# Expert products on TensorE in the order of their weights, and the sums of x and the expert outputs on VectorE, each tile's transposes beside its sums

## The chip, the cores and the metric

One core of a Trainium2 chip runs the whole kernel. The metric is device time in microseconds. The kernel before took 1904.27 us as the median of three runs (1900.39 to 1905.04); less is better.

## The reference, cut to what matters

Two transformer blocks run one after the other on 512 tokens of width 1024, in fp32. The change lies at the seam between them: the mixture of experts that ends the first block, the sum of its output with x, and the normalisation with which the second block begins.

```python
def hierarchical_moe(h, ...):
    ...
    for e in range(N_EXPERTS):
        hid = jax.nn.silu(jnp.matmul(h, w_gate[e])) * jnp.matmul(h, w_up[e])
        out = out + jnp.matmul(hid, w_down[e]) * combine[:, e:e + 1]
    return out

    m = hierarchical_moe(h2, ...)
    return x + m.reshape(b, s, d)          # end of the first block
    ...
    h = rms_norm(x, norm_gain[l])          # start of the second block
    cols = h @ w_in_a[j]
    ...
    mem_out = memory_cross_attention(q_mem, mem, ..., w_mem_kv[l], ...)
```

There are 32 experts. A token goes to two of them, so its output is the sum of two rows, and x + m is a sum of three terms.

## The kernel before, in words

Products of full precision are split in three: each fp32 operand is written as a high and a low part (names `whi`, `wlo` for weights, `hh`, `hl` for activations), and `mm3` (lines 368 to 372) issues three matmuls, high by high (L370), low by high (L371), high by low (L372). The high part of a weight unit is made by ScalarE (L229), the low part by VectorE or GpSimd (L232). The experts' products are the exception: they take the raw fp32 weights.

All weights come from HBM through one class, `Stream`. A plan lists the units (mostly 512 KB) in the order of use, SyncE issues their loads as soon as a slot of the unit's lane is free (L217), and `ws.get` hands them out in the order of the plan. The lanes have names such as `mraw`, `hraw`, `xraw`, `praw`; in the expert loop they hold dozens of units at the start and, towards the end, mainly those of `mraw` (twelve slots), `hraw` and `xraw`. Slots of `xraw` are also where the four tiles of x (`x<-x1d`, L1468) are put after the loop, and slots of `mraw` hold the tiles `m` and `gF` of the stage behind it.

**The expert loop** (lines 1448 to 1464). Experts are handled in 16 pairs; 64 tokens of the one and 64 of the other share a tile of 128. For a pair, `gather_tokens` (L1374 to L1384) fetches the tokens' rows by an indirect DMA from GpSimd, scales them on VectorE (L1377), transposes them on TensorE (eight transposes, L1382) and copies them back (L1384). `gate_up` (L1397) uses eight weight units in four steps u0 to u3; `hidden` (L1402 to L1404) forms the gated product `th` on ScalarE and VectorE; `turned` (L1410) transposes it twice; `down` (L1423) uses four units, in two halves that ScalarE (L1427) and VectorE (L1425) copy to `y`, of which there are two tiles; GpSimd then scatters `y` by rows to `yd` in HBM (L1428). The weights are planned in the order: units 0 to 7 of pair j+1, then units 8 to 11 of pair j. So `gate_up` of the next pair comes ahead of `down` of this one. The program is written in that order too, with the gather of pair j+1 ahead of its own `gate_up`, but on TensorE a scheduler picks the final order by its own estimates.

**After the loop.** A count decides whether up to fourteen additional pairs are needed. `values_load` (L1511) brings it into a register of every engine (a TENSOR_LOAD on each), and a branch (L1516) skips the additional code; with this data it is always skipped. Behind the branch each engine goes on in the second section of the program, and the order there on TensorE, ScalarE, VectorE and GpSimd is the written one (`manual_schedule`):

- `vB_steps`, 16 `mm3` of the memory tokens with the value weights, of which `AFTER[0]` steps are issued ahead of the loads of `m` and the rest behind.
- SyncE loads eight tiles from `yd`: `ms[c]` (L1530) and `ms2[c]` (L1531), the two expert rows of the tokens of tile c. They wait until the last scatter is in HBM.
- `kv`, 16 `mm3` with the key weights (`acc<-whi,mT`), dealt out by the numbers of `AFTER`.
- for each tile c of 128 tokens: `x2[c] += ms2[c]` on GpSimd (L1537), `x2[c] += ms[c]` on VectorE (L1538), and the sum of squares of the result on ScalarE (L1542). ScalarE and GpSimd also split the first four weight units of the second block in between (`kraw`, L229 and L232).
- at c = 3, `transposed` turns all four tiles: six transposes for each tile into six PSUM banks (L401), then the other eight (L409), each followed by the high and low part (`hh` by L383, `hl` by L384). The first product of the second block is `sc<-whi,hh`.

## Time and profile before

| what | value |
|---|---|
| median of three runs | 1904.27 us (1900.39 to 1905.04) |
| the profiled execution | 1904.58 us |
| its span, first to last instruction | 1902.8 us |
| mean granted TensorE clock | 0.976 of full speed |
| busy share | TensorE 95%, VectorE 47%, ScalarE 39%, GpSimd 20% |
| bytes moved | 261.17 MB |

The profiled execution lies 0.3 us above the median. All times below are counted from the start of its span. The expert loop's first product comes at 491 us and its last ends at 744 us, and the second block's first product stands at 811 us. The stage between, in which x + m is formed, is the one in which TensorE idles most: a page that calls it 95% busy overall says little about it.

### The profile page before, as it was taken

The numbers are of one execution on the slowest core, as the hardware profiler recorded it, in microseconds if no ns is written. First come the engines' busy times: TensorE is split into PE (matmuls) and PEld (weight loads), VectorE is DVE, ScalarE is ACT, GpSimd is POOL, SyncE is SP. The second block draws the span as 40 slices with busy tenths as digits, with TensorE's granted clock in tenths as the row PEclk, the third lists the DMA queues.
The fourth block names the chain that finished last, engine by engine and source line by source line (L and its number), as shares of the span: only waits on it lengthen the run. The fifth ranks groups of instructions, "written<-read, shape, count | busy, mean of one in ns | idle before, by whom it ended". The sixth has DMA issues, their size and how long they took to land.

```text
span 1902.8 us, 25340 instructions
## 1 busy us (share of the span) xinstructions
PE 1806.9 (95%) x9426; PEld 1384.7 (73%) x9426; DVE 888.2 (47%) x1876; ACT 733.6 (39%) x1754; POOL 378.4 (20%) x467
## 2 busy tenths in 40 slices
PE   8999999998997787499999999999999999999999
PEld 8857766786432223389989889989888877777887
DVE  4389756276322231262243332243466426677571
ACT  5475355243100111243454433454454333233460
POOL 1301200010210101422533302433300001222200
PEclk9999999999999798799999999999999999999999
DMA  5221222187999996442222212222223322112231
GB/s 176 78 67 34 72 69 81 50 279 275 380 415 412 412 399 234 157 136 89 89 67 89 67 45 92 85 67 89 67 89 112 133 66 92 65 58 66 67 111 56
DMA packets 83685, 261.17 MB, mean 137 GB/s; under 512 B 12896, under 2 KB 14688, under 8 KB 83552
## 3 DMA queue, kind: packets, MB, share of 16 engines
q1 hardware_dynamic: 78080, 248.43, 36.9%
q0 software_dynamic: 4608, 8.40, 1.2%
q10 hardware_dynamic: 864, 2.62, 0.3%
q8 instruction: 77, 1.26, 0.3%
q14 instruction: 56, 0.46, 0.1%
HBM read 248.92 MB, written 18.87 MB: 141 GB/s over the span
## 4 chain that ended last, share of the span: by engine, by line
PE 56%; DVE 2%; issue 1%; ACT 1%; POOL 1%; POOLq 0%; ACTq 0%
PE acc L370 14%; PE acc L371 13%; PE acc L372 13%; PE sc L370 2%; PE sc L372 2%; PE sc L371 2%; PE sc L1916 1%; PE sc L1712 1%; PE tp L1653 1%; PE sc L1715 1%; PE tp L1720 1%; PE oT L1729 1%; PE oT L1964 1%; POOL x L1537 0%; PE oT L1724 0%
## 5 line engine op out<-in xcount | busy, mean ns | idle before, releaser
L370 PE MATMUL acc<-whi,hh 128*128 128x512 f32 (+2 forms) x936 | 383.0, 411 | 1.4 <-ACT hh L383 0.6
L371 PE MATMUL acc<-wlo,hh 128*128 128x512 f32 (+2 forms) x936 | 372.6, 399 | 0.0
L372 PE MATMUL acc<-whi,hl 128*128 128x512 f32 (+2 forms) x936 | 371.8, 400 | 0.0
L232 DVE TENSOR_TENSOR wlo<-wraw,whi 128x1024 fp32r<-128x1024 f32 (+4 forms) x209 | 244.9, 1175 | 252.0 <-ACT whi L229 251.2
L229 ACT ACTIVATE whi<-wraw 128x1024 fp32r<-128x1024 f32 (+4 forms) x239 | 239.2, 1002 | 296.8 <-PE acc L371 115.8
L370 PEld LDWEIGHTS acc<-whi,hh 128*128 128x128 f32 x936 | 223.5, 239 | 28.0 <-issue 2.8
L371 PEld LDWEIGHTS acc<-wlo,hh 128*128 128x128 f32 x936 | 224.1, 240 | 22.1 <-issue 1.7
L372 PEld LDWEIGHTS acc<-whi,hl 128*128 128x128 f32 x936 | 222.9, 239 | 21.6
L370 PE MATMUL acc<-hh,whi 128*128 128x512 f32 x448 | 184.7, 412 | 0.0
L372 PE MATMUL acc<-hh,wlo 128*128 128x512 f32 x448 | 177.7, 397 | 0.0
L371 PE MATMUL acc<-hl,whi 128*128 128x512 f32 x448 | 176.8, 395 | 0.0
L232 POOL TENSOR_TENSOR wlo<-wraw,whi 128x1024 fp32r<-128x1024 f32 (+3 forms) x30 | 70.6, 2353 | 526.6 <-ACT whi L229 452.2
L365 POOL TENSOR_TENSOR rs<-rsa,mhalf 128x4 f32<-128x4 f32 (+1 forms) x80 | 79.2, 990 | 325.7 <-DVE rsa L362 269.3
L1397 PE MATMUL acc<-mraw,xgt 128*64 128x512 f32 x232 | 103.0, 649 | 6.5 <-DMA mraw<-in_w_moe 5.5
L704 ACT ACTIVATE hjk<-acc 128x128 bf16<-128x128 f32 x232 | 64.1, 276 | 104.2 <-PE acc L372 73.2
L370 PEld LDWEIGHTS acc<-hh,whi 128*128 128x128 f32 x448 | 84.5, 189 | 21.2 <-issue 4.9
L372 PEld LDWEIGHTS acc<-hh,wlo 128*128 128x128 f32 x448 | 84.2, 188 | 19.8 <-issue 1.0
L371 PEld LDWEIGHTS acc<-hl,whi 128*128 128x128 f32 x448 | 84.6, 189 | 15.5
L1403 DVE SCALAR_TENSOR_TENSOR th<-th,acc 128x256 f32<-128x256 f32 x16 | 6.7, 420 | 129.6 <-ACT th L1402 129.6
L707 DVE TENSOR_TENSOR nat<-acc,rs 128x512 f32<-128x512 f32 x52 | 35.9, 691 | 61.3 <-POOL rs L365 43.4
L1397 PEld LDWEIGHTS acc<-mraw,xgt 128*64 128x64 f32 x232 | 28.0, 147 | 43.8 <-issue 32.2
L371 PE MATMUL sc<-wlo,hh 128*128 128x512 f32 (+2 forms) x144 | 55.9, 389 | 0.0
(546 smaller groups left out, 3180.5 us busy)
## 6 DMA issues: line engine op xcount, KB each, us to landing
mraw<-in_w_moe SPq DMA_DIRECT2D x86, 512.0 KB
wraw<-in_w_qka SPq DMA_DIRECT2D x48, 512.0 KB
xraw<-in_w_moe SPq DMA_DIRECT2D x25, 512.0 KB
hraw<-in_w_moe SPq DMA_DIRECT2D x44, 256.0 KB
praw<-in_w_moe SPq DMA_DIRECT2D x22, 512.0 KB
qraw<-in_w_moe SPq DMA_DIRECT2D x21, 512.0 KB
wraw<-in_w_va SPq DMA_DIRECT2D x20, 512.0 KB
wraw<-in_w_qfb SPq DMA_DIRECT2D x16, 512.0 KB
```

Of the source, the lines that this page charges most:

```text
L229: nc.scalar.activation(hi, raw, AF.Copy)
L232: eng.tensor_tensor(lo, raw, hi.bitcast(F32), OP.subtract)
L365: G.tensor_tensor(r[:, :m], t[:, :m], mhalf[:, :m], OP.pow)
L370: T.matmul(p, a[0], b[0], start=start, stop=False)
L371: T.matmul(p, a[0], b[1], start=False, stop=False)
L372: T.matmul(p, a[1], b[0], start=False, stop=stop)
L704: S.activation(jk, p[:, h * 128:h * 128 + 128], AF.Square, accum_out=st[:, h:h + 1])
L707: V.tensor_tensor(t.rearrange("p (h d) -> p h d", h=nh), p.rearrange("p (h d) -> p h d", h=nh), r[:, :nh, None].to_broadcast([128, nh, 128 ...
L1397: T.matmul(p[z], X[2 * u + k][:, z], w[e][k], start=u + k == 0, stop=u + k == 4)
L1653: T.transpose(tp[:, c * 128:c * 128 + 128], nat[c][:, j * 128:j * 128 + 128], ident)
L1712: T.matmul(p[32 * j:32 * j + 32, :256], q0[:, 128 * j + c:128 * j + 128:4], k0[:, 128 * BASE[j]:128 * BASE[j] + 256], start=True, stop=True)
L1715: T.matmul(p[:, 128 + g * 128:256 + g * 128], qk[g][s][:, cs], qk[g][2 + s][:, cs], start=True, stop=True)
```

## The change

1. In the expert loop TensorE is under `manual_schedule`, so its instructions stand in the order written. They are written in the order of the weights: `gate_up` of pair j+1 (u0 to u2), the eight transposes of the tokens of pair j+2, the two of `turned` of pair j, u3 of pair j+1, `down` of pair j. The tokens are gathered one pair earlier than before.
2. `values_load` of the count moves from behind the loop into it, at j = 14. On TensorE its TENSOR_LOAD then stands ahead of the last pair's `turned` and `down`; on VectorE, ScalarE and GpSimd it still stands behind the last copy of `y` or the last scatter.
3. In the stage after the branch all steps of `vB_steps` are pumped behind the loads of `m`. Both sums of a tile are on VectorE, `ms` first and `ms2` second. `transposed` gets an argument `before`, called ahead of each tile's six transposes: it issues some `kv` steps, the two sums and the sum of squares. The numbers of `AFTER` become (5, 3, 3, 3, 1): five steps of `kv` ahead of tile 0, three between tiles.

```diff
--- before.py
+++ after.py
@@ -276,7 +276,7 @@
 
 
 ROUTER = (1, 1, 1, 2, 4, 4, 8)
-AFTER = (8, 4, 4, 4, 2, 2)
+AFTER = (5, 3, 3, 3, 1)
 
 FILL = (4, 4, 4, 3, 3, 3, 3)
 
@@ -392,11 +392,14 @@
             S.activation(junk[:, :n], x, AF.Square, accum_out=ss[:, c:c + 1])
         return rsq(pool, ss[:, :len(xs)], n)
 
-    def transposed(xs, gain, pool, tag, bufs, nk=8, banks=(), tps=None, more=None):
+    def transposed(xs, gain, pool, tag, bufs, nk=8, banks=(), tps=None, more=None, before=None):
+
 
         w = 128 * len(xs)
         tps = tps or [bank() for bank in banks]
         for c, x in enumerate(xs):
+            if before:
+                before(c)
             for k, tp in enumerate(tps):
                 T.transpose(tp[:, c * 128:c * 128 + 128], x[:, k * 128:k * 128 + 128], ident)
         res = []
@@ -1445,23 +1448,37 @@
         S.activation(t, p, AF.Copy)
         nc.sync.dma_start(kvd[:, 1024 + 512 * c:1536 + 512 * c], t)
 
-    pg = acc()
-    gate_up(ws.get, Xg, pg, range(4))
-    for j in range(16):
-        th = hidden(pg, cw[:, j:j + 1])
+
+
+    def tokens(j):
+        return gather_tokens(j, idx[:, j:j + 1], rw[:, j:j + 1])
+
+    order = ExitStack()
+    order.enter_context(tc.manual_schedule(engines={mybir.EngineType.PE}))
+    pg, Xnext = acc(), None
+    for j in range(-1, 16):
+        if j >= 0:
+            th = hidden(pg, cw[:, j:j + 1])
         if j == 8:
             mT = mem_load(mo)
             vB_steps = memory_steps(ws, mT, store_v, (scp, otp))
         if j < 15:
-            Xg = gather_tokens(j + 1, idx[:, j + 1:j + 2], rw[:, j + 1:j + 2])
-            pg = acc()
+            Xg = Xnext or Xg
+            pg = acc() if j >= 0 else pg
             gate_up(ws.get, Xg, pg, range(3))
-        t = turned(th)
+        if j < 14:
+            Xnext = tokens(j + 2)
+        if j >= 0:
+            t = turned(th)
         if j < 15:
             gate_up(ws.get, Xg, pg, range(3, 4))
-        down(ws.get, t, odx[:, j:j + 1])
+        if j >= 0:
+            down(ws.get, t, odx[:, j:j + 1])
         if j == 0:
             pump(kv)
+        if j == 14 and not dbg.get("noif"):
+            nv = nc.values_load(next_i[0:1, 0:1], min_val=0, max_val=14)
+    order.close()
 
     x2 = [xtile("x2") for _ in range(4)]
     for c in range(4):
@@ -1508,7 +1525,6 @@
         down(get, turned(hidden(p, w[:, 0:1])), ox)
 
     if not dbg.get("noif"):
-        nv = nc.values_load(next_i[0:1, 0:1], min_val=0, max_val=14)
         more = ExitStack()
         for e in range(14):
             more.enter_context(tc.If(nv > e))
@@ -1524,22 +1540,21 @@
     ET = mybir.EngineType
     with tc.manual_schedule(engines={ET.PE, ET.Activation, ET.DVE, ET.Pool}):
         kmB = [mo.tile([128, 512], F32, name="kmB", tag="mraw", bufs=MR) for _ in range(2)]
-        pump(vB_steps, AFTER[0])
         ms, ms2 = ([big("m", "mraw", MR) for c in range(4)] for _ in range(2))
         for c in range(4):
             nc.sync.dma_start(ms[c], yd[128 * c:128 * c + 128, :])
             nc.sync.dma_start(ms2[c], yd[512 + 128 * c:640 + 128 * c, :])
+        pump(vB_steps)
         kv = mem_k(1, mT, mo, lambda j: kmB[j])
-        pump(vB_steps)
         tps = [bank() for bank in (scp, scp, scp, otp, tpp, tpp)]
-        for c in range(4):
-            pump(kv, AFTER[c + 1])
-            G.tensor_tensor(x2[c], x2[c], ms2[c], OP.add)
+
+        def add_experts(c):
+            pump(kv, AFTER[c])
             V.tensor_tensor(x2[c], x2[c], ms[c], OP.add)
+            V.tensor_tensor(x2[c], x2[c], ms2[c], OP.add)
             tap("x2", x2[c], c)
-            if c == 3:
-                hT = transposed(x2, gFA, hp_, "h", 16, tps=tps, more=scp)
             S.activation(ms[c], x2[c], AF.Square, accum_out=s3[:, c:c + 1])
+        hT = transposed(x2, gFA, hp_, "h", 16, tps=tps, more=scp, before=add_experts)
         for c in range(4):
             m = ms[c]
             (G if c < 1 else V).tensor_tensor(m, x2[c], gF, OP.mult)
@@ -1549,7 +1564,7 @@
         V.tensor_scalar(a12[:, 0], s4, 1.0 / 1024, None, OP.mult)
         V.scalar_tensor_tensor(a12[:, 0], a12[:, 1], EPS, a12[:, 0], op0=OP.mult, op1=OP.add)
         G.tensor_tensor(r12, a12, mhalf.rearrange("p (a c) -> p a c", a=2), OP.pow)
-        pump(kv, AFTER[5])
+        pump(kv, AFTER[4])
     norm_tiles(mo, r12[:, 0], True)
     pump(kv)
     for j in range(2):
```

**TensorE, end of the expert loop.** `mraw`, `hraw` and `xraw` are weight units, `acc` the bank of `gate_up`, `sc` that of `down`; a pair's `down` is eight instructions (each stands for the matmuls of both experts of the pair). Before, from the last `gate_up` on:

```order
L1397 MATMUL acc<-mraw,xgt 64x512 x4
L1410 MATMUL tp<-c_ident,th 128x128 x2
L1423 MATMUL sc<-mraw,hid 64x512
L1423 MATMUL sc<-hraw,hid 64x512
L1423 MATMUL sc<-mraw,hid 64x512
L1423 MATMUL sc<-hraw,hid 64x512
L1423 MATMUL sc<-mraw,hid 64x512 x4
L1423 MATMUL sc<-xraw,hid 64x512
L1423 MATMUL sc<-mraw,hid 64x512
L1423 MATMUL sc<-xraw,hid 64x512
L1423 MATMUL sc<-mraw,hid 64x512 x5
```

In the changed kernel, the program's last rows ahead of the branch:

```order
L1400 MATMUL acc<-mraw,xgt 64x512 x4
L1426 MATMUL sc<-mraw,hid 64x512 x4
L1426 MATMUL sc<-hraw,hid 64x512
L1426 MATMUL sc<-mraw,hid 64x512
L1426 MATMUL sc<-hraw,hid 64x512
L1426 MATMUL sc<-mraw,hid 64x512
L1480 TENSOR_LOAD nexti
L1413 MATMUL tp<-c_ident,th 128x128 x2
L1426 MATMUL sc<-mraw,hid 64x512 x5
L1426 MATMUL sc<-hraw,hid 64x512
L1426 MATMUL sc<-mraw,hid 64x512
L1426 MATMUL sc<-hraw,hid 64x512
```

Before, 28 instructions of `down`, three pairs and a half, follow the last of `gate_up` (the first fifteen are shown). In the changed kernel 16 do, the last eight of them being the last pair's, and the load of the count (TENSOR_LOAD) stands ahead of those eight.

**TensorE, the stage after the branch.** The four numbered names `x_...` are the four tiles of x2, `mT` the memory tokens. Before, the last `kv` step and the transposes:

```order
L370 MATMUL acc<-whi,mT 128x512
L371 MATMUL acc<-wlo,mT 128x512
L372 MATMUL acc<-whi,mT 128x512
L401 MATMUL sc<-c_ident,x_6092 128x128 x3
L401 MATMUL oT<-c_ident,x_6092 128x128
L401 MATMUL tp<-c_ident,x_6092 128x128 x2
L401 MATMUL sc<-c_ident,x_6093 128x128 x3
L401 MATMUL oT<-c_ident,x_6093 128x128
L401 MATMUL tp<-c_ident,x_6093 128x128 x2
L401 MATMUL sc<-c_ident,x_6094 128x128 x3
L401 MATMUL oT<-c_ident,x_6094 128x128
L401 MATMUL tp<-c_ident,x_6094 128x128 x2
```

In the changed kernel, the third tile's transposes and the three `kv` steps ahead of them:

```order
L370 MATMUL acc<-whi,mT 128x512
L371 MATMUL acc<-wlo,mT 128x512
L372 MATMUL acc<-whi,mT 128x512
L370 MATMUL acc<-whi,mT 128x512
L371 MATMUL acc<-wlo,mT 128x512
L372 MATMUL acc<-whi,mT 128x512
L370 MATMUL acc<-whi,mT 128x512
L371 MATMUL acc<-wlo,mT 128x512
L372 MATMUL acc<-whi,mT 128x512
L404 MATMUL sc<-c_ident,x_6111 128x128 x3
L404 MATMUL oT<-c_ident,x_6111 128x128
L404 MATMUL tp<-c_ident,x_6111 128x128 x2
```

The six transposes of a tile, which stood together with those of the other tiles behind all but two `kv` steps, now each have three `kv` steps ahead of them.

**GpSimd, the same stage.** `kraw` are the second block's first weight units. Before:

```order
L232 TENSOR_TENSOR wlo<-kraw,whi 128x1024
L1537 TENSOR_TENSOR x_6092<-x_6092,m 128x1024
L232 TENSOR_TENSOR wlo<-kraw,whi 128x1024
L1537 TENSOR_TENSOR x_6093<-x_6093,m 128x1024
L232 TENSOR_TENSOR wlo<-kraw,whi 128x1024
L1537 TENSOR_TENSOR x_6094<-x_6094,m 128x1024
L232 TENSOR_TENSOR wlo<-kraw,whi 128x1024
L1537 TENSOR_TENSOR x_6095<-x_6095,m 128x1024
L1545 TENSOR_TENSOR m<-x_6092,gF 128x1024
```

In the changed kernel:

```order
L232 TENSOR_TENSOR wlo<-kraw,whi 128x1024 x4
L1560 TENSOR_TENSOR m<-x_6109,gF 128x1024
L232 TENSOR_TENSOR wlo<-wraw,whi 128x1024
L1566 TENSOR_TENSOR r_8696<-a_8695,mhalf 128x8
L365 TENSOR_TENSOR rs<-rsa,mhalf 128x4 x2
```

The four sums are gone from between the four low parts; on VectorE eight sums now stand in a row, two for a tile, behind the last three low parts of the `kv` weights.

## Rows read from the trace of the kernel before

**Rows 1.** The page, memory traffic in GB/s over 40 slices of 47.6 us.

```profile
GB/s 176 78 67 34 72 69 81 50 279 275 380 415 412 412 399 234 157 136 89 89 67 89 67 45 92 85 67 89 67 89 112 133 66 92 65 58 66 67 111 56
```

**Rows 2.** Busy time by windows: stretch, its length, busy of each engine, PEclk, DMA share, GB/s.

```profile
610.00:640.00 30.00, 16.58 (x50) 4.69 (x50) 3.74 (x7) 1.47 (x4) 2.00 (x2) 0.79 1.03 411
```

**Rows 3.** TensorE's waits, 490 to 745 us: us in total, times, longest.

```profile
PE tp L1382 <- DVE xg L1377: 5.6, 4, 2.3
```

**Rows 4.** The same windows view around the last weights and the first products behind the branch.

```profile
730.00:732.00 2.00, 2.00 (x6) 0.51 (x6) 0.00 (x0) 0.00 (x0) 0.00 (x0) 0.50 0.95 381
732.00:734.00 2.00, 2.00 (x8) 0.52 (x6) 0.63 (x1) 0.60 (x1) 0.95 (x1) 0.73 0.20 82
...
752.00:757.00 5.00, 4.99 (x12) 3.94 (x13) 0.00 (x0) 0.00 (x0) 0.97 (x1) 0.50 0.19 66
```

**Rows 5.** TensorE's timeline, 587 to 812 us: start, length, instruction, idle time before.

```profile
587.23 1.06 PE L1382 MATMUL tp<-c_ident,xg 128*128 128x128 f32 x8 [0.52 <-DVE xg L1377]
...
728.34 0.44 PE L1410 MATMUL tp<-c_ident,th 128*128 128x128 f32 x2 [1.45 <-DVE th L1404]
...
733.15 1.88 PE L1423 MATMUL sc<-mraw,hid 128*64 128x512 f32 x8
...
743.35 0.59 PE L1423 MATMUL sc<-hraw,hid 128*64 128x512 f32 x1
752.01 0.77 PE L370 MATMUL sc<-whi,mT 128*128 128x512 f32 x1 [8.07 <-DVEq L1516]
...
765.58 0.40 PE L370 MATMUL acc<-whi,mT 128*128 128x512 f32 x1
...
766.28 0.39 PE L370 MATMUL acc<-whi,mT 128*128 128x512 f32 x1
...
804.92 0.90 PE L401 MATMUL sc<-c_ident,x 128*128 128x128 f32 x3 [8.68 <-DVE x L1538]
...
811.29 0.54 PE L370 MATMUL sc<-whi,hh 128*128 128x512 f32 x1
```

**Rows 6.** GpSimd's timeline, 752 to 817 us.

```profile
752.68 0.97 POOL L1428 DMA_INDIRECT yd<-y,v0o  x1 [3.90 <-DMA yd<-y,v0o]
772.48 2.39 POOL L232 TENSOR_TENSOR wlo<-kraw,whi 128x1024 fp32r<-128x1024 f32 x1 [18.83 <-ACT whi L229]
774.84 2.35 POOL L1537 TENSOR_TENSOR x<-x,m 128x1024 f32<-128x1024 f32 x1
...
801.45 2.34 POOL L1545 TENSOR_TENSOR m<-x,gF 128x1024 f32<-128x1024 f32 x1
813.26 3.93 POOL L232 TENSOR_TENSOR wlo<-wraw,whi 128x1024 fp32r<-128x1024 f32 x1 [9.48 <-ACT whi L229]
```

**Rows 7.** VectorE's timeline, 747 to 815 us.

```profile
747.09 0.69 DVE L1425 COPY y<-sc 128x512 f32<-128x512 f32 x1 [5.03 <-PEq L1516]
...
764.06 1.23 DVE L232 TENSOR_TENSOR wlo<-wraw,whi 128x1024 fp32r<-128x1024 f32 x1 [1.59 <-ACT whi L229]
777.23 1.22 DVE L1538 TENSOR_TENSOR x<-x,m 128x1024 f32<-128x1024 f32 x1 [11.94 <-POOL x L1537]
...
801.52 3.35 DVE L1538 TENSOR_TENSOR x<-x,m 128x1024 f32<-128x1024 f32 x1 [6.88 <-POOL x L1537]
...
811.43 3.49 DVE L1545 TENSOR_TENSOR m<-x,gF 128x1024 f32<-128x1024 f32 x3
```

**Rows 8.** ScalarE's timeline: the first high part of the next weights.

```profile
771.34 1.06 ACT L229 ACTIVATE whi<-kraw 128x1024 fp32r<-128x1024 f32 x1 [4.96 <-DMA kraw<-in_w_va]
```

**Rows 9.** SyncE's timeline: the last load of x, the first of m, those of the next weights.

```profile
736.78 0.33 SPq L1468 DMA_DIRECT2D x<-x1d  x1
...
757.29 0.33 SPq L1530 DMA_DIRECT2D m<-yd  x1
...
761.69 3.95 SPq L217 DMA_DIRECT2D kraw<-in_w_va  x3
```

**Rows 10.** DMA view, 726 to 760 us, GpSimd's queue (six scatters): packets, MB, share.

```profile
q0 software_dynamic: 864, 1.58, 12.5%
```

## The prediction

> **What bounds the kernel now.** I read the page's memory traffic first, then windows over the expert loop and its end, then the waits, and last the timelines of the five queues from the end of the loop to the first product of the second block.
>
> The traffic row shows the expert loop: for four slices, from about 490 to 700 us, it stands at 412 to 415 GB/s, and nowhere else is it near that [rows 1]. In a window of this stretch TensorE is busy 16.58 of 30 us while memory still gives 411 GB/s [rows 2]. So the loop is bound by its weights: no order on TensorE makes it faster as long as slots come free early enough. TensorE's waits there for the gathered tokens are small (5.6 us in four) [rows 3].
>
> The stage behind the loop is another matter. The weights' traffic falls from 381 to 82 GB/s between 730 and 734 us [rows 4], so the last weight is there at about 732. From then on nothing comes from the plan that TensorE needs, yet the second block's first product stands at 811.29 [rows 5]: 79 us, in which memory is mostly idle. What follows is therefore a chain of work and waits, and it is this chain that the change shortens. After 811 I see no reason for the rest to change, so a gain at this product is taken to be a gain in the end.
>
> The chain before, in its links: TensorE does what is left of `down` (until 743.94), VectorE's last copy of `y` stands at 747.09 and the branch lets TensorE go on at 752.01 [rows 5, 7]. Then 13.6 us of `vB_steps`, the first 5 us of them at half clock [rows 4, 5], and `kv`. The last scatter is only issued at 752.68, since it waits for an earlier one to land; the loads of `m` follow at 757.29 [rows 6, 9]. From 772.48 a ring of 8.1 us turns four times: GpSimd's low part (2.39), GpSimd's sum (2.35), VectorE's sum (1.22), ScalarE's squares and the next high part (1.06), which the next low part waits for [rows 6 to 8]. It ends with the fourth tile's transposes at 804.92 [rows 5]; `hh`, `hl`, the other transposes and two `kv` steps take 6.4 us more, to 811.29.
>
> **The order of the weights.** *The last weight.* What landed behind the last weight before must now go ahead of it: one load of x, 0.52 MB, issued at 736.78 before because its slot was held by a late `down` [rows 9], and four of the five scatters issued behind 732. Six scatters moved 1.58 MB [rows 10], so 0.26 MB each: in all 1.57 MB, which at 411 GB/s [rows 2] is 3.8 us. The last weight moves from 732.2 to **736.0** (bounds: 732.2 if none of it comes in front, 738.6 if a scatter costs as much as its whole tile of 0.52 MB).
>
> A page of the Trainium skill, "DMA: Bandwidth & Descriptors" (section "Where 436 GB/s comes from"), puts the limit of loads from HBM at about 358 GB/s for a core; the trace differs with its 411 GB/s, so I go by the trace. By the page's figure the term would be an estimated 4.4 us.
>
> *The last products.* In order, only the second half of the last `down` is left when the last unit lands, eight of its sixteen matmuls. At full clock eight take 1.88 us [rows 5], at half clock twice that; with the landing itself I take 2.5. TensorE is through at **738.5** in place of 743.94 (bounds 735 to 742).
>
> *The branch.* Before, the copies of the last pair stood 3.1 us behind their product, I take it because the scatter two pairs earlier still held one of the two tiles of `y`, as these copies all fell into the last 18 us. In order they come a pair of weights apart, 16 us, so I take 0.2 us. Then the copy, 0.69, and from its end (747.78) to the first product (752.01) 4.2 us for the load of the count and fifteen branches [rows 5, 7]. That stays, since only TensorE's own load of the count moves ahead: VectorE's and ScalarE's remain behind their copies. So `vB_steps` begin at 738.5 + 5.1 = **743.6**, 8.4 us sooner, and end 13.6 us later at 757.2.
>
> *The loads of m.* The last scatter can go at 739.5, as no other is in its way. From its issue (752.68) to the first load of `m` it was 4.6 us [rows 6, 9]: now 744. Eight loads of 0.52 MB take 10.2 us at 411 GB/s, so all of `m` is there by 754.3, ahead of its first use.
>
> *Moved for nothing.* The gathers are issued one pair earlier; GpSimd sits idle most of the loop (2.00 of 30 us [rows 2]), so nothing queues behind them. TensorE's eight transposes are the same number. If a pair's tokens come late all the same, it is paid once for a pair: that is a rival, below.
>
> **The sums.** Four sums leave GpSimd (2.35 each [rows 6]) and four come to VectorE (1.22 each [rows 7]); with that the ring is gone, because no low part of `kraw` waits for a sum any more on GpSimd. VectorE's queue now: three low parts of the `kv` weights, then eight sums. The third low part ended 13.3 us after the first product of `vB_steps` (764.06 + 1.23 against 752.01 [rows 5, 7]), so now at 756.9.
>
> - Bound from below: eight sums at 1.22 take 9.8 us, to 766.7. TensorE is then the later one: `kv` at 0.70 a step (765.58 to 766.28 [rows 5]), 14 steps from 757.2 make 767.0, and three tiles' transposes lie between, six to a tile and 0.8 us by the eight that took 1.06 [rows 5]: 769.4. With the 6.4 us of the tail the first product stands at **775.8**.
> - Bound from above: GpSimd works on four low parts of `kraw` in the same stretch, 2.39 each [rows 6]. Where a VectorE sum and a GpSimd operation on two tiles began together (801.52 and 801.45) the sum took 3.35 in place of 1.22 [rows 6, 7]: it stood until GpSimd was through. If all four low parts stop the sums so, these end at 766.7 + 9.4 = 776.1 and the product stands at **782.5**.
>
> Between these I take three stops. The first two low parts are ready when `kraw` lands: 14 us after the first load of `m` before (757.29 to 771.34, where ScalarE waited for it [rows 8, 9]), so about 758, when the sums have just begun. The third waits on ScalarE for the second tile's squares, the fourth for the third tile's; by then the last sums are nearly through. 766.7 + 3 x 2.34 = 773.7, and with 6.4 us the first product stands at **780.1**, 31.2 us sooner.
>
> The Trainium skill says in "GPSIMD Engine Reference" (section "Key points") that GpSimd shares its SBUF interfaces with VectorE and collides with VectorE instructions that have two SBUF inputs. This speaks against putting all sums on VectorE beside GpSimd's low parts. It says neither who goes first nor what a collision costs; the row of 3.35 us is the one that has a price.
>
> **The sum.** 1904.6 of the profiled execution (0.3 above the median) less 31.2 makes 1873.4: I say **1873**. In parts: 8.4 us from the earlier start behind the branch, the other 22.8 from the ring.
>
> **The rivals.**
>
> *No collision.* When GpSimd began at 813.26 while VectorE was at three operations in a row (811.43 to 814.92), it was GpSimd that took 3.93 and VectorE lost nothing [rows 6, 7]. If a queue of sums keeps the way free like that, the product stands at the lower bound, 775.8: 35.5 us sooner, **1869**. For it speaks that the sums are in a row; against it that the row of 3.35 shows the reverse when GpSimd is first.
>
> *The loop's end does not move.* The order does not do what it says where it matters: the last weight, at half clock, or the copies' lag takes back the 5.4 us, and `vB_steps` still start near 752. Then the third low part ends at 765.3, the last `m` is there at 767.5, the sums end at 775.1 plus three stops, 782.1, and the product stands at 788.5: 22.8 us sooner, **1882**. For it: the clock is at 0.50 just there [rows 4], and with the loop in order TensorE pauses more.
>
> *Slower: TensorE becomes the bound of the loop.* In a fixed order one late piece (tokens, `th`, a bank of `down`) stops every product behind it, the slots are not freed, and the loads stop. A pair's twelve units, 6.3 MB, and its gather and scatter, 0.53 MB, take 16.6 us at 411 GB/s. Its TensorE work is 48 matmuls at 0.235 (1.88 for eight) and ten transposes, 1.06 for eight and 0.44 for two [rows 5]: 12.8 us at full clock, so 3.8 us are to spare. It decides from stalls of s us a pair with 16 x (s - 3.8) > 31.2 + 5.7, that is s above 6.1; at 8 us it would cost 67 us, less the gain of 31, and give **1940**. Against it: all of the gathers' waits together were 5.6 us before [rows 3], and the slots hold more than a pair of weights in front. Half clock would double the work, but a busy TensorE was back at full clock after 5 us [rows 4, 5].
>
> **How the numbers follow.** My forecast has 0.48, no collision 0.22, the loop's end in place 0.22, slower 0.05, and 0.03 is for stalls that just eat the gain. A change of this kernel shows in a measurement from about 0.3%, 5.7 us. Faster by more is thus 0.92, the same 0.03, slower 0.05. The range reaches from 1862 (no collision, and the last products at their lower bound of 735, 3.5 us sooner, with another 3.5 for smaller things) to 1889 (the loop's end in place with a fourth stop, 1884.6, and a late `kraw`). It holds the first three cases but for their tails.
>
> **What the profile would show.** Traffic at about 411 GB/s up to 736 and TensorE's last `down` by 738.5; the first product of `vB_steps` near 743.6, after a wait for the branch; the first load of `m` near 744; sums of 1.22 us with three of about 3.4 among them; waits for sums ahead of a tile's transposes of a few us at most, in place of 8.68 at the fourth tile [rows 5]; `sc<-whi,hh` near 780. Wrong it would be if the loop's traffic sank below 400 GB/s, if waits of TensorE for tokens or `th` came once for a pair, if the branch took more than 5 us, or if time that is gained before 780 comes back behind it because the second block's weights are not yet split.

## The result, and the profile after

The changed kernel takes 1872.96 us (median of four runs, 1872.17 to 1873.79), against 1904.65 for the kernel before beside it: a ratio of 0.9839, with a 95% interval of 0.9821 to 0.9856. That is 31.7 us less, and 1873 had been forecast. The profiled execution took 1873.42 us with a span of 1871.6, 31.2 below the span before. The 31.2 us of the forecast are met to a tenth, but that is luck: several of its terms were off by 2 to 5 us, and the errors went against each other.

TensorE's timeline of the changed kernel, from the last expert products to the first product of the second block, answers to [rows 5]:

```profile
734.95 4.39 PE L1426 MATMUL sc<-mraw,hid 128*64 128x512 f32 x9 [2.30 <-DMA mraw<-in_w_moe]
...
740.32 0.59 PE L1426 MATMUL sc<-hraw,hid 128*64 128x512 f32 x1
744.88 0.52 PE L370 MATMUL sc<-whi,mT 128*128 128x512 f32 x1 [3.96 <-DVEq L1532]
...
771.38 0.55 PE L404 MATMUL sc<-c_ident,x 128*128 128x128 f32 x3 [1.69 <-DVE x L1554]
...
773.92 1.97 PE L412 MATMUL sc<-c_ident,x 128*128 128x128 f32 x8 [1.67 <-DVE hl L384]
...
778.25 0.63 PE L370 MATMUL sc<-whi,hh 128*128 128x512 f32 x1
```

The reader is to see three starts: the first product behind the branch at 744.88 (752.01 before), the fourth tile's transposes at 771.38 (804.92), the first product of the second block at 778.25 (811.29). So the first product behind the branch stands 7.1 us sooner, and 25.9 us are gained between there and the first product of the second block, 33.0 in all. The span shows 31.2; 1.8 us are lost behind that. Not all of the 7.1 us are the loop's doing. Its own first product, behind code that is the same in both kernels, already stood 2.1 us sooner in this execution (the first row is of before):

```profile
491.12 3.65 PE L1397 MATMUL acc<-mraw,xgt 128*64 128x512 f32 x16 [0.35 <-DVE xgt L1384]
489.06 5.37 PE L1400 MATMUL acc<-mraw,xgt 128*64 128x512 f32 x24 [0.35 <-DVE xgt L1387]
```

Over the thirteen traces of this study that product stands anywhere from 487.44 to 491.27. From it to the first product behind the branch the loop took 260.9 us before and takes 255.8 now, 5.1 less. The waits of TensorE from 780 us to the end name one that the kernel before did not have:

```profile
PE tp L697 <- DVE mkn L710: 1.7, 1, 1.7
```

The windows view around the last weights, answering to [rows 4], and two windows of the stage behind (columns as there; PEclk stands ahead of the DMA share):

```profile
734.00:736.00 2.00, 1.05 (x2) 0.29 (x2) 0.00 (x0) 0.00 (x0) 0.00 (x0) 0.73 0.41 158
736.00:738.00 2.00, 2.00 (x7) 0.75 (x5) 0.00 (x0) 0.00 (x0) 0.97 (x1) 0.50 0.06 27
772.00:776.00 4.00, 2.33 (x12) 2.09 (x11) 2.89 (x5) 3.97 (x8) 4.00 (x3) 0.56 0.55 179
776.00:780.00 4.00, 4.00 (x12) 3.09 (x12) 1.16 (x2) 1.47 (x2) 2.56 (x2) 0.59 0.56 182
```

The weights now end near 735, some 2.5 us later than before by the trace and some 5 counted from the loop's first product. A load of x and three scatters that came behind them now go ahead; two scatters are still issued behind (736.63 and 742.44 below). TensorE waits 2.30 us for the last weights and then works at half clock (0.50).

The timelines of VectorE, GpSimd, ScalarE and SyncE in the stage behind the branch, in that order, answer to [rows 6 to 9]:

```profile
741.00 0.69 DVE L1428 COPY y<-sc 128x512 f32<-128x512 f32 x1 [8.00 <-PE sc L1426]
...
757.36 1.22 DVE L1553 TENSOR_TENSOR x<-x,m 128x1024 f32<-128x1024 f32 x1
...
764.54 3.43 DVE L1553 TENSOR_TENSOR x<-x,m 128x1024 f32<-128x1024 f32 x1
768.01 3.31 DVE L1554 TENSOR_TENSOR x<-x,m 128x1024 f32<-128x1024 f32 x1
```

```profile
736.63 0.97 POOL L1431 DMA_INDIRECT yd<-y,v0o  x1 [6.99 <-DMA yd<-y,v0o]
742.44 0.97 POOL L1431 DMA_INDIRECT yd<-y,v0o  x1 [4.84 <-DVE y L1428]
764.45 11.41 POOL L232 TENSOR_TENSOR wlo<-kraw,whi 128x1024 fp32r<-128x1024 f32 x4 [21.04 <-ACT whi L229]
```

```profile
763.31 1.06 ACT L229 ACTIVATE whi<-kraw 128x1024 fp32r<-128x1024 f32 x1 [4.78 <-DMA kraw<-in_w_va]
765.24 1.06 ACT L229 ACTIVATE whi<-kraw 128x1024 fp32r<-128x1024 f32 x1 [0.87 <-DMA kraw<-in_w_va]
...
771.36 1.06 ACT L1556 ACTIVATE m<-x 128x1024 f32<-128x1024 f32 x1
...
772.41 1.82 ACT L383 ACTIVATE hh<-sc,gFA 128x512 fp32r<-128x512 f32 x3
```

```profile
748.86 0.33 SPq L1545 DMA_DIRECT2D m<-yd  x1
```

Six of the eight sums take 1.22 us, one behind the other. The last two take 3.43 and 3.31: they are the two that fall beside GpSimd's low parts, which begin at 764.45. ScalarE has four high parts of `kraw` and the squares of four tiles ahead of the first `hh`, and from 765.24 on it works through them without a pause. The last sum is through at 771.32 and the fourth tile's squares begin at 771.36, when ScalarE comes free: the sums and ScalarE's queue end together here.

### The profile page after: what moved, and what is told of

Its sections match the earlier page's. It is cut to its first block, busy times and chain, and to the rows that moved or that the text cites. A ratio compares the mean times of both kernels' runs of the same rounds, so it can differ in the third digit from the quotient of the medians.

```text
span 1871.6 us, 25322 instructions
## 1 busy us (share of the span) xinstructions
PE 1791.2 (96%) x9426; PEld 1381.5 (74%) x9426; DVE 894.3 (48%) x1880; ACT 733.9 (39%) x1754; POOL 368.0 (20%) x463
## 4 chain that ended last, share of the span: by engine, by line
PE 85%; DMA 9%; DVE 3%; ACT 2%; issue 1%; SPq 0%; POOL 0%; POOLq 0%; ACTq 0%; DVEq 0%
PE acc L370 19%; PE acc L372 18%; PE acc L371 18%; PE acc L1400 3%; PE sc L370 3%; PE sc L371 3%; PE sc L372 3%; DMA mraw<-in_w_moe 3%; DMA hraw<-in_w_moe 2%; PE sc L1931 1%; PE sc L1426 1%; PE sc L911 1%; PE sc L1727 1%; DMA xraw<-in_w_moe 1%; PE tp L1668 1%; PE oT L936 1%
## 5 line engine op out<-in xcount | busy, mean ns | idle before, releaser
L1400 PE MATMUL acc<-mraw,xgt 128*64 128x512 f32 x232 | 95.5, 621 | 0.3 <-DVE xgt L1387 0.3
L370 PE MATMUL sc<-whi,hh 128*128 128x512 f32 (+2 forms) x144 | 55.7, 392 | 0.0
L372 PE MATMUL sc<-whi,hl 128*128 128x512 f32 (+2 forms) x144 | 55.0, 388 | 0.0
```

What stands on the lines that cost most here:

```text
L370: T.matmul(p, a[0], b[0], start=start, stop=False)
L372: T.matmul(p, a[1], b[0], start=False, stop=stop)
L1400: T.matmul(p[z], X[2 * u + k][:, z], w[e][k], start=u + k == 0, stop=u + k == 4)
```

## The experiments

Theory: two gains that add, the order of the weights (an earlier start) and the sums taken out of GpSimd's ring. Times are medians; each is set against the kernel before, measured beside it.

**One half of the change at a time.** In the first kernel the loop is the changed one and the stage behind it that of before:

```diff
-        hT = transposed(x2, gFA, hp_, "h", 16, tps=tps, more=scp, before=add_experts)
+        for c in range(4):
+            pump(kv, AFTER[c + 1])
+            G.tensor_tensor(x2[c], x2[c], ms2[c], OP.add)
+            V.tensor_tensor(x2[c], x2[c], ms[c], OP.add)
...
```

> The changed expert loop with the stage of before behind it. My account (the two parts add): the first product behind the branch starts near 745 as in the changed kernel, the ring of 8.1 us a tile still turns four times but begins about 8 us sooner, so the first product of the second block stands near 803 and the time is about 1896.5, 8 us under before. Rival (the order of the weights gives nothing by itself, the ring begins when its own weights land): 1903 to 1905. Rival (the order is the main part): 1885 or less.

Measured: 1895.57, 7.4 us under before (ratio 0.9958, interval 0.9942 to 0.9975). TensorE's waits from 735 to 815 us, and the three starts:

```profile
PE sc L404 <- DVE x L1554: 25.1, 4, 8.7
```

```profile
744.10 0.69 PE L370 MATMUL sc<-whi,mT 128*128 128x512 f32 x1 [4.03 <-DVEq L1532]
...
796.04 0.90 PE L404 MATMUL sc<-c_ident,x 128*128 128x128 f32 x3 [8.68 <-DVE x L1554]
...
802.32 0.39 PE L370 MATMUL sc<-whi,hh 128*128 128x512 f32 x1
```

The ring is whole (25.1 us of waits in four) and lies 8.9 us sooner in the trace; 2.8 of these were there at the loop's first product (488.37), and the loop took 255.7 us for 260.9. The second kernel has the loop of before and the changed stage:

```diff
-    for j in range(-1, 16):
+    for j in range(16):
...
```

> The expert loop and the place of the count's load as before, with the changed stage behind it. My account: the first product behind the branch stays at 752, the first product of the second block comes 33.4 us later as in the changed kernel, at 785.5, and the time is about 1880.5, 24 us under before. Rival (the changed stage pays only when the loads of m come early): 1888 or more. Rival (all of the gain is in the stage): 1873.

Measured: 1880.24, 22.7 us under before (0.9883, interval 0.9866 to 0.9900). Two starts of TensorE, the only sum that was stopped, and ScalarE's first `hh`:

```profile
749.14 0.76 PE L370 MATMUL sc<-whi,mT 128*128 128x512 f32 x1 [7.79 <-DVEq L1518]
...
784.60 0.63 PE L370 MATMUL sc<-whi,hh 128*128 128x512 f32 x1
```

```profile
770.89 3.30 DVE L1540 TENSOR_TENSOR x<-x,m 128x1024 f32<-128x1024 f32 x1
```

```profile
778.77 1.82 ACT L383 ACTIVATE hh<-sc,gFA 128x512 fp32r<-128x512 f32 x3
```

The product stands near the 785.5 expected, but by two misses that cancel: the start was 749.14 and not 752 (2.8 of that at the loop's first product, 488.32), and the way from there 35.5 us and not 33.4. The sums are not what made the way longer. They end at 774.2; `hh` waits for ScalarE, which reaches the fourth tile's squares at 777.73, behind four high parts, of which the second and the fourth waited for their loads.

Together 7.4 and 22.7 make 30.1 of the 31.7: the halves add within their intervals, and neither needs the other. The forecast's price for the stage alone had been 22.8.

**What in the stage pays.** The sum of `ms2` goes back to GpSimd, the transposes stay beside the sums:

```diff
-            V.tensor_tensor(x2[c], x2[c], ms2[c], OP.add)
+            G.tensor_tensor(x2[c], x2[c], ms2[c], OP.add)
```

> The changed kernel with the sum of ms2 back on GpSimd, everything else as changed. My account: on GpSimd the sums stand between the low parts of kraw again, the fourth tile is summed near 791 and the first product of the second block stands near 798, so 1893. Rival (it is the place of the transposes and of kv that gains, not the engine of the sum): at most 1877.

Measured: 1898.72, only 4.2 us under before (0.9978, interval 0.9966 to 0.9991): less than the order alone gives. GpSimd's timeline tells why:

```profile
764.49 4.64 POOL L232 TENSOR_TENSOR wlo<-kraw,whi 128x1024 fp32r<-128x1024 f32 x2 [19.78 <-ACT whi L229]
769.09 4.63 POOL L1553 TENSOR_TENSOR x<-x,m 128x1024 f32<-128x1024 f32 x2
781.53 2.38 POOL L232 TENSOR_TENSOR wlo<-kraw,whi 128x1024 fp32r<-128x1024 f32 x1 [7.81 <-ACT whi L229]
```

The first sum waits behind two low parts, the third low part 7.81 us for its high part, and TensorE reaches the fourth tile's transposes at 799.63. The expected 1893 had a ring of the old pace; that ScalarE's changed order slows it is my reading of these waits, not a run of its own. Against the changed kernel, from which this one differs by one engine's name, it is 25.8 us by the medians. In the other run the transposes are all put behind the fourth sum:

```diff
-        hT = transposed(x2, gFA, hp_, "h", 16, tps=tps, more=scp, before=add_experts)
+        for c in range(4):
+            add_experts(c)
+        hT = transposed(x2, gFA, hp_, "h", 16, tps=tps, more=scp)
```

> The changed kernel with all four tiles' transposes behind the fourth sum, as before. My account: the sums end at 771 as now, then TensorE has 24 transposes in place of six, 2.4 us more, so 1875.4. Rival (the transposes beside the sums keep TensorE busy and its clock up, which is worth more): 1879 or more. Rival (they are hidden either way behind the high and low parts of h): 1873.

Measured: 1874.42 (0.9850, interval 0.9834 to 0.9867), which can't be told from the changed kernel. In its trace the first three tiles' transposes are done from 767 to 769, while VectorE is still at the fourth tile's sums, and the fourth's wait about as in the changed kernel (1.66 for 1.69), so they are hidden either way:

```profile
771.01 0.55 PE L404 MATMUL sc<-c_ident,x 128*128 128x128 f32 x3 [1.66 <-DVE x L1554]
```

The engine of the sum is the gain; the place of the transposes is worth nothing that can be measured. Putting all of `vB_steps` behind the loads of `m`, the third part of the change in this stage, was not tried by itself.

**The load of the count** goes back behind the loop:

```diff
-        if j == 14 and not dbg.get("noif"):
-            nv = nc.values_load(next_i[0:1, 0:1], min_val=0, max_val=14)
```

> The changed kernel with the load of the count behind the loop again, as before. My account: VectorE's load of the count behind its last copy sets the branch, TensorE's is hidden beside it, so the first product behind the branch stays at 745 and the time at 1873. Rival (the place of TensorE's load is what shortens the branch from 4.2 us behind the copy to 3.2): 1 us later, 1874. Rival (the moved load is much of the gain at the start): 1876 or more.

Measured: 1873.14 (0.9839, interval 0.9826 to 0.9852), no difference. VectorE's last copy and TensorE's first product behind the branch:

```profile
743.93 0.69 DVE L1428 COPY y<-sc 128x512 f32<-128x512 f32 x1 [7.61 <-PE sc L1426]
```

```profile
747.62 0.77 PE L370 MATMUL sc<-whi,mT 128*128 128x512 f32 x1 [3.79 <-DVEq L1531]
```

TensorE goes on 3.0 us behind the copy's end, about as with the load moved (741.69 to 744.88). The profiled execution of this kernel took 1879.05 us, 6 above the median, and differs in the stage too: three sums are stopped in it (3.32, 3.42 and 3.25), ScalarE waits 3.12 us for the last, and the first product stands at 784.27.

**The stops.** The first experiment on them puts `kraw`'s parts off, the low parts on GpSimd and with them the high parts on ScalarE. `may` says how many of them may be issued:

```diff
+            ws.may = max(0, c - 1)
+            ws.advance()
...
+        ws.may = 4
+        ws.advance()
```

> The changed kernel with the high and low parts of kraw put off: the first behind the third tile's squares, the second behind the fourth's, the others behind the parts of h. The fourth tile's two sums, 3.43 and 3.31 in the changed kernel, should take 1.22 each. My account: TensorE's own work then sets the fourth tile's transposes, so only the wait of 1.7 us ahead of them goes: 1871.3. Rival (the stops cost their whole 4.3 us): 1868.7. Rival (the late parts are then waited for by the first products): 1876 or more.

Measured: 1876.97 (0.9857, interval 0.9843 to 0.9871), 4 us slower than the changed kernel. Rows of TensorE, ScalarE, VectorE and of TensorE's waits (735 to 830 us):

```profile
774.01 0.39 PE L372 MATMUL sc<-whi,hh 128*128 128x512 f32 x1
```

```profile
769.94 1.84 ACT L385 ACTIVATE hh<-sc,gFA 128x512 fp32r<-128x512 f32 x3 [0.67 <-PE sc L406]
```

```profile
775.94 9.94 DVE L1566 TENSOR_TENSOR m<-x,gF 128x1024 f32<-128x1024 f32 x3
```

```profile
PE tp L699 <- DVE mkn L712: 3.4, 1, 3.4
```

The windows view of the same run:

```profile
772.00:776.00 4.00, 4.00 (x21) 3.26 (x20) 4.00 (x8) 4.00 (x7) 0.30 (x1) 1.00 0.58 165
776.00:780.00 4.00, 4.00 (x19) 3.26 (x18) 4.00 (x3) 1.52 (x2) 4.00 (x2) 1.00 0.24 42
```

The stops at the sums are gone and the first product comes 4.2 us sooner, more than the wait of 1.69 us ahead of the transposes. This does not show that the stops cost 4.2 us, since the high parts went from ScalarE's queue as well. Of the 4.2, 2.5 are an earlier `hh` (769.94 for 772.41), which now waits for the transposes and no longer for the queue. The other 1.7 lie between `hh` and the product, 4.1 us for 5.8; TensorE is at full clock from 772 to 780, where it had 0.56 and 0.59. Whether stops or queue set the first product is read from two other traces, at the end of this section.

In this run the late low parts meet the three products m x gF, which take 9.94 in place of some 3.5 to 3.9; the norm is late, and TensorE waits for it. The next run puts the last two parts behind the norm:

```diff
-        ws.may = 4
-        ws.advance()
...
+        ws.may = 4
+        ws.advance()
         pump(kv, AFTER[4])
```

> As the run in which kraw's parts were put off, but the last two pairs of parts stand behind the whole reckoning of the norm on ScalarE and GpSimd, so that neither its products m x gF nor its power wait for them. My account now: the stops cost 4.2 us at the first product of the second block (778.25 to 774.0), and it was the norm, late by 6 us, that took them back. So 1868 to 1869. Rival (a later product waits for the third or fourth low part): 1872 or more. Rival (the time is set elsewhere and nothing of the 4.2 us comes through): 1873.

Measured: 1874.68 (0.9845, interval 0.9829 to 0.9862). The first product is at 773.97 again, and the meeting has moved on, to the scale R (0.17 in the changed kernel) and to x r gF (3.67):

```profile
782.74 2.32 DVE L430 COPY R<-r 128x4 f32<-128x4 f32 x1 [1.78 <-POOL r L1570]
784.97 7.98 DVE L1579 SCALAR_TENSOR_TENSOR x<-x,r,gF 128x1024 f32<-128x1024 f32 x3
```

So the last rival holds: nothing of the 4.2 us came through, since in both places tried the low parts met VectorE's work on SBUF and cost there. One place is free, between the last sum and m x gF, where VectorE makes the low parts of h from PSUM. The last of these runs puts three parts there and the fourth on VectorE, and holds back the parts of the weight that comes next until those are issued:

```diff
-            ws.may = max(0, c - 1)
+            ws.may = (0, 0, 1, 3)[c]
...
-        ws.may = 4
+        ws.may, ws.vec = 4, True
+        ws.advance()
+        ws.vec, ws.stop = False, 1 << 30
...
-        eng = nc.gpsimd if every and self.count[tag] % every == 0 else nc.vector
+        eng = nc.gpsimd if every and self.count[tag] % every == 0 and not self.vec else nc.vector
```

> The changed kernel with three of kraw's low parts on GpSimd right behind the last sum, while VectorE makes the low parts of h (one operand of those comes from PSUM, and they took 0.69 us each beside a working GpSimd before, as without), the fourth on VectorE once the norm is reckoned, and the next weight's behind that. My account: a GpSimd operation only costs where VectorE has two SBUF operands, and the earlier runs moved it from the sums to m x gF and to x r gF; here one such meeting is left. First product of the second block at 774, VectorE's scale R by 785, and the time 1869. Rival (another meeting takes it back again, at x r gF): 1873 or more.

Measured: 1870.44 (1865.95 to 1871.04; 0.9816, interval 0.9799 to 0.9833), 2.5 us under the changed kernel by the medians, and 33.3 under the kernel before beside it, where the changed kernel has 31.7. Every run lies below every run of the changed kernel; the two intervals against before still overlap. GpSimd, VectorE and TensorE's waits (735 to 850 us):

```profile
766.74 7.11 POOL L235 TENSOR_TENSOR wlo<-kraw,whi 128x1024 fp32r<-128x1024 f32 x3 [23.47 <-ACT whi L232]
```

```profile
783.03 5.84 DVE L1582 SCALAR_TENSOR_TENSOR x<-x,r,gF 128x1024 f32<-128x1024 f32 x3
```

```profile
PE tp L701 <- DVE mkn L714: 0.3, 1, 0.3
```

Three low parts take 7.11, no more than 2.37 each, while VectorE is idle or makes low parts of h, which keep their length. One meeting is left (5.84), and the late wait is down to 0.3. It is the fastest kernel of the study by its median; what the held-back weight has in that was not tried alone.

**More of the loop.** Two attempts to use TensorE's idle time in the loop failed. The first puts the memory tokens' value products into pairs 12 to 14:

```diff
+            if j in (13, 14):
+                pump(vB_steps, 4 if j == 13 else None)
...
+        if j in (12, 13):
+            pump(vB_steps, 4)
```

> The changed kernel with the 16 products of the memory tokens with the value weights put into the expert loop, a quarter at a time around pairs 12 to 14, and their weights planned there. My account says that the stage behind the branch is a chain of TensorE's own work, and that TensorE has several us to spare for each pair in the loop: kv then begins right behind the branch, the loads of m set the sums, and the first product of the second block comes about 9 us sooner, 1864. Rival (the loads of m and of kraw bind at once): 1870. Rival (the products in the loop hold up the experts, the last weight comes later): 1875 or more.

Measured: 1875.36 (0.9847, interval 0.9835 to 0.9860). TensorE is busy nearly without a gap from 725 to 742 us, the last copies of `y` fall together again, and the branch opens late. VectorE's last copy, which stands at 745.65, waited 5.51 us for a scatter. TensorE's first product behind the branch:

```profile
755.69 0.77 PE L370 MATMUL acc<-whi,mT 128*128 128x512 f32 x1 [7.45 <-DVEq L1537]
```

The second writes out the order of ScalarE and VectorE too:

```diff
-    order.enter_context(tc.manual_schedule(engines={mybir.EngineType.PE}))
+    order.enter_context(tc.manual_schedule(engines={mybir.EngineType.PE, mybir.EngineType.Activation, mybir.EngineType.DVE}))
...
+        if j == 15:
+            ws.stop = 1 << 30
+            ws.advance()
```

> The changed kernel with ScalarE and VectorE also in the written order in the expert loop, and the parts of the weights for the memory tokens put off to the last pair; so part of those weights is loaded behind the experts' last one. In the changed kernel VectorE stood at such a part (14.4 us, from 667 to 682), TensorE idled 10 us behind it and memory fell to 346 GB/s for a while. My account: that stall goes (2 us), 2.5 MB or 6 us of loads move behind the last expert weight, VectorE's load of the count comes ahead of its last copy; the first product behind the branch stands at 737 to 740 in place of 745, and the time at 1867. Rival (what follows waits for those weights instead): 1873 or more. Rival (VectorE and ScalarE in order hold up the experts): 1878 or more.

Measured: 1880.52 (0.9880, interval 0.9863 to 0.9896). TensorE's waits in the loop and at its end, and the window in which memory traffic fell to 332 GB/s:

```profile
PE tp L1387 <- DVE xg L1382: 36.6, 1, 36.6
```

```profile
PE sc L1428 <- ACT hid L1417: 8.5, 1, 8.5
```

```profile
640.00:670.00 30.00, 23.37 (x102) 9.09 (x104) 9.78 (x15) 4.62 (x8) 4.49 (x5) 0.80 0.90 332
```

VectorE, in written order, stands at the parts of the memory tokens for 36 us with the tokens' scaling behind it; ScalarE holds the last pair's `hid` behind the weights' high parts. This is the slower rival of the forecast come true, on other engines. With this edit and the earlier run's parts behind the norm in one kernel:

> Both of the two runs above in one. If they add: 4 and 6 us under the changed kernel, 1863. If the loads of m and kraw bind instead once the start is earlier: the better of the two alone, 1867 to 1869.

Measured: 1878.89 (0.9871, interval 0.9853 to 0.9890). The two don't add; the loop's loss remains.

**Stops or queue.** In the run with the stage alone one sum is stopped, and in the one with all orders written out none is. There the last sum, the first row here, is through at 769.8, and ScalarE's first `hh` still comes at 777.68:

```profile
768.61 1.23 DVE L1559 TENSOR_TENSOR x<-x,m 128x1024 f32<-128x1024 f32 x1
```

```profile
777.68 1.82 ACT L384 ACTIVATE hh<-sc,gFA 128x512 fp32r<-128x512 f32 x3
```

From `kraw`'s first high part to the first `hh` it is 9.3 us with no sum stopped, 9.9 with one, 9.1 with two (the changed kernel) and 12.3 with three (the run with the count late). So with up to two stops ScalarE's queue sets the first product, and only with a third do the sums. What two stops cost by themselves, with the queue left as it is, no run measures; these traces leave next to nothing for them.

## Why the prediction was right, and where it was not

*The last weight* (736.0 forecast, 3.8 us later than before): near 735 in the trace, but some 5 us later than before when both are counted from the loop's first product. *The last products* (738.5): TensorE was through at 740.91. The step that failed is "only the second half of the last `down` is left when the last unit lands": all sixteen matmuls were, as TensorE waited 2.30 us for the first half's weights, and half clock made them 6 us long. *The branch* (5.1 us): 4.0, as the copy stood right behind its product and the way from the copy to the product was 3.2 in place of 4.2. The lag of 3.1 went as argued. That 1.0 is not explained by the place of the count's load. The way was 4.2 to 5.1 in the three traces in which ScalarE's and VectorE's last copies stand together (before, the stage alone, the values in the loop) and 2.4 to 3.3 in all others; the cause stays open.

The start came 7.1 us sooner, for 8.4 forecast, but only 5.1 of it is the loop's: 4.1 from copies and branch, and 1.0 from the products, which the forecast had 5.4 us sooner. The other 2.1 lie ahead of the loop, where the kernels are the same.

*The loads of m* (744): 748.86. The scatter was issued 3 us late with the products, and took 6.4 us to the first load, where 4.6 had been taken from [rows 6, 9]. This moved `kraw` from 758 to 763.31, and with it the stops: two sums met a low part, not three, and the sums ended at 771.3 in place of 773.7. The meeting's price was as in [rows 7], 3.4 for 1.22. Here the term "766.7 + 3 x 2.34" was mis-sized by one stop. How many there are goes with how far `kraw` comes behind the first sum: three at 4.7 us (the count late), two at 6.0 (the changed kernel), one at 6.4 (the stage alone), none at 8.2 (all orders written out).

*From the last sum to the product* 6.4 us were taken from before, and that step failed too: it put ScalarE's queue ahead of `hh` at nothing. It measured 6.9. `hh` began 1.03 us behind the start of the fourth tile's transposes, 0.51 before, as the squares of that tile now stand ahead of it; from `hh` to the product it was 5.8 us in both, at about half clock (0.56 and 0.59; 0.50 before). That this cost 0.5 us and no more is luck, since sums and queue ended together. By the traces with one stop and with none, fewer stops would hardly have brought the product sooner while the high parts stayed ahead of `hh`. It stood at 778.25 for 780.1.

*After the first product* nothing had been forecast; 1.8 us were lost there to a late norm, whose scale R was copied 10.6 us behind the product, 8.0 before. So 3.3 us less from the loop, 2.1 more from ahead of it, 3.1 more in the stage and 1.8 lost behind it left about nothing. Of the claims behind the sum the two that carry it are shown by runs: the halves add (7.4 and 22.7), and the ring is broken by the engine of the sum, not by the place of the transposes.

*The rivals.* No collision: refuted, two sums were stopped. Without stops the first product stood at 774.0, close to the 775.8 of the bound, but in a run that also shortens ScalarE's queue. The row that spoke for this rival was misread: beside the GpSimd operation at 813.26 VectorE did lose something, on the operation right behind the three, which before takes 0.16 us where it stands alone (817.14):

```profile
814.84 2.38 DVE L1548 TENSOR_SCALAR a<-s 128x4 f32<-128x4 f32 x1
```

The loop's end in place: refuted by the run with the order alone, whose loop took 255.7 us for 260.9. (The end of the range that goes with this rival should read 1884.2 for 1884.6; nothing hangs on it.) Slower: not here, though two of the signs named for it came. TensorE waited for the gathered tokens once for a pair, 14 times, of which two were long (21.4 and 10.0 us):

```profile
PE tp L1413 <- DVE xgt L1387: 35.5, 14, 21.4
```

And the traffic sank below 400 GB/s in one window of 30 us, 385 from 670 to 700; in all others memory held 407 to 417. There VectorE had a weight's low part ahead of the tokens' scaling:

```profile
682.43 1.23 DVE L232 TENSOR_TENSOR wlo<-wraw,whi 128x1024 fp32r<-128x1024 f32 x1 [14.36 <-ACT whi L229]
```

By these two rates that window cost some 2 us, (412 - 385) x 30 / 412. Before, the last two such windows held 397 and 405, some 1.6 us by the same reckoning, so little of it is lost against before. No run undid it cleanly, so whether it can be had back stays open.

The rule on the shared interfaces ("GPSIMD Engine Reference" of the Trainium skill, section "Key points") was borne out by the trace: 3.43 and 3.31 us beside a working GpSimd, 1.22 without. The 358 GB/s from HBM that the Trainium skill gives for a core ("DMA: Bandwidth & Descriptors", section "Where 436 GB/s comes from") were exceeded again, with 407 to 417 in all windows of the loop but one.

## What to carry to other kernels

Where two engines alternate in a ring, look for the operation of the slower one that can leave it: one sum in a different queue was worth 25.8 us, the place of the transposes around it nothing. A wait names what came last; before calling that the cause, look at what else would have held the instruction (here ScalarE's queue, through at the same moment as the sums), and at what else an edit moves that takes the wait away. Where two engines shut each other out of SBUF, moving one's work does not remove its cost but hands it to the next place where both are busy; look for the stretch in which the other reads PSUM or is idle. And an order written out for one engine is safe only as long as no other queue has a late piece ahead of an early one.

## What the runs showed of the hardware

A VectorE operation on two SBUF operands that met a GpSimd operation stood until that was through (3.43 and 3.31 us for 1.22), and GpSimd was held up as well: four low parts took 11.41 us beside two stopped sums, and 9.61 in the run with all orders written out, where no sum was stopped beside them. Work of one SBUF operand stood too: a copy of 128 x 4 took 2.32 for 0.17. VectorE's low parts of h, with an operand in PSUM, kept their length beside GpSimd, and so did a GpSimd product m x gF beside them (2.43). With the clock at 0.56 and 0.59 the way from `hh` to the first product took 5.8 us, with it at 1.00 some 4.1; TensorE had paused 1.69 and 1.67 us on the longer way, not at all and 1.02 on the shorter. The way from a scatter's issue to the first load that needs it, for the same 0.26 MB, was 4.3 to 4.6 us in three traces (before, the stage alone, the values in the loop) and 5.2 to 6.6 in the others; the cause is open.
